# Running sum of three block products in one accumulator bank, at the end of a transformer layer kernel

## The chip, the cores and the metric

The kernel runs on one core of one Trainium2 chip. The engines are TensorE (PE, matrix products into the accumulator memory PSUM), VectorE (DVE, two-input element-wise work), ScalarE (ACT, one-input element-wise work), GpSimd (POOL) and SyncE (SP, which here only issues transfers). Each engine works through its own queue in order, and the queues are kept apart by semaphores. The metric is the device time of one execution in microseconds; times are medians of several runs, and one execution is also recorded by the hardware profiler.

## The reference

One layer on 512 tokens of width 1024, in float32: RMSNorm, a wide projection, three branches (gated linear attention, forgetting attention, attention into 256 memory tokens), merged by gates and projected; then a feed-forward layer and a last RMSNorm. What matters here is the end:

```python
u2 = rmsnorm(h, g_ffn[l])
h = h + jnp.square(jax.nn.relu(u2 @ w_ff1[l])) @ w_ff2[l]     # w_ff1 (1024, 4096), w_ff2 (4096, 1024)
return rmsnorm(h, g_final)
```

## The kernel before

**Precision.** Every float32 operand is split into a high and a low part (`split`, lines 207 to 209: ScalarE casts `hi` on line 208, VectorE subtracts to get `lo` on line 209), and `mm3` (line 154) multiplies by three matmuls: high by high (line 155), high by low (156), low by high (157). Weights pass through `wp`, a pool with three slots each for raw, `hi` and `lo`, so the cast of a tile waits until TensorE has done with the tile three places before.

**Feed-forward layer.** The 4096 hidden channels are worked in four quarters, q = 0 to 3. In each, `first_product` makes the hidden activations, and `second_product` (line 1338) multiplies them by the quarter's rows of `w_ff2` and adds to the result `hN`: four tiles of 128 tokens by 1024. Both are 2 by 2 block products by Winograd's form of Strassen's method: seven block products instead of eight. `C(i, j, t)` is the part of the result in token half i, column half j, tile t of that half, 128 by 512.

**Second product.** The block products are made in the order `SECOND` = 1, 2, 5, 3, 6, 7, 4. Their left factors are sums of activation blocks (`left`, `late_left`), their right factors sums of weight blocks: `factor` (line 1329) lets a GpSimd-issued transfer add the next block in DRAM onto the tile that is in SBUF (`b11`, `b12`) and splits it (`split_b`, line 1153); products 2 and 3 use plain blocks (`ring`). A block product is made for two token tiles t = 0, 1 and two halves of the contraction i = 0, 1: 24 matmuls of 128 by 512, ordered i = 0 (t = 0, then t = 1), then i = 1 (t = 0, then t = 1). Only the very last one (q = 3, n = 4) goes t = 0 with both i first, then t = 1. Each (product, t) has a PSUM bank. Products 1 and 5 stay in two banks each of pool `pa` (tiles `a`, kept in `held`) and are summed there by TensorE over all four quarters; all others get a fresh bank (`mmt`, tile `mm`, four of them) and are read out by `evac` (line 1286):

- products 2 and 3 are added to C(0,0) and C(0,1), product 4 to C(1,0), in every quarter;
- products 6 and 7 are collected in `R6` and `R7` in the first three quarters; R7 is added to C(1,0) and taken from C(1,1) before the last quarter's second product;
- in the last quarter product 1 is copied out by ScalarE, added to C(0,0), and R6 is subtracted from it; at product 6 this gives E (the sum of products 1 and 6 over all quarters, with sign) and G = held product 5 - E. Then C(0,1) += G, C(1,1) += G, C(1,0) += E. Product 7 is taken from C(1,1) and added to C(1,0).

**Finishing.** `finish(t, c, n)` (line 1269) is called when a half row of the result is final. It squares and sums the half on ScalarE; on the first half (n = 0) it multiplies it by the last gain; on the second (n = 1) it forms the reciprocal root (VectorE line 876, GpSimd `pow` line 877), scales both halves (VectorE line 1278, ScalarE line 1280) and stores them from the SP queue (line 1279) and the ScalarE queue (line 1281). Tiles 0 and 1 become final with product 6, tiles 2 and 3 with product 4.

**Order of work.** TensorE's order is the order of the code (`manual_schedule`, line 1470). For all other engines a planner orders the instructions at build time by simulating a timeline, and inserts the waits; `tc.issue_after(x)` makes what follows on the same engine come behind instruction x in that order, without waiting for its end.

Of the kernel before, what the change touches and what calls it, by code (L numbers as in the profile page):

```python
# [9 lines left out]
F32 = mybir.dt.float32  # L10
# [4 lines left out]
ALU = mybir.AluOpType  # L15
AX = mybir.AxisListType

P = 128
# [46 lines left out]
def hybrid_block(ctx, tc, chunks, wst, memT, xN, cols, gffn, gfin, wup, cst, out):  # L65
    nc = tc.nc
# [5 lines left out]
    def nm(s):  # L72
        uid[0] += 1
        return f"{s}_{uid[0]}"
# [10 lines left out]
    def mmt(shape=None):  # L85
        return pmm.tile(shape or [P, 512], F32, tag="mm", name=nm("mm"))

    def at_(shape=None):
        return pa.tile(shape or [P, 512], F32, tag="a", name=nm("a"))

    def f(ap):
        return ap.bitcast(F32)
# [58 lines left out]
    def get_w(key):  # L151
        return split_w(load_w(key))

    def mm3(ps, lh, ll, rh, rl, start, stop):
        nc.tensor.matmul(ps, lh, rh, start=start, stop=False)  # L155
        nc.tensor.matmul(ps, lh, rl, start=False, stop=False)  # L156
        nc.tensor.matmul(ps, ll, rh, start=False, stop=stop)  # L157

    def gT(key, rhi, rlo, evac, n=S):

# [46 lines left out]
    def split(hi, lo, src):  # L207
        nc.scalar.copy(hi, src)  # L208
        return nc.vector.tensor_tensor(lo, src, f(hi), op=ALU.subtract).ins  # L209
# [41 lines left out]
    with pool("front") as fp:  # L251
# [25 lines left out]
        ps = at_()  # L277
# [7 lines left out]
        for j in range(4):  # L285
            for k in (2 * j, 2 * j + 1):
                with tc.issue_after(act):
                    act = nc.scalar.mul(mxh[:, k, :], memr[:, k, :], gmem[:, k:k + 1]).ins
                nc.vector.scalar_tensor_tensor(mxl[:, k, :], memr[:, k, :], gmem[:, k:k + 1], f(mxh[:, k, :]),
                                               op0=ALU.mult, op1=ALU.subtract)  # L290
# [62 lines left out]
        for k in range(KT):  # L353
# [3 lines left out]
            if k in (3, 5):  # L357
                h = k // 5
# [508 lines left out]
    def sumsq(sq, src, t, c, n):  # L867

        nc.scalar.activation(sq, src[:, 512 * c:512 * c + 512], AF.Square, accum_out=hss[:, t, n:n + 1])
        if n == 0:  # L870
            nc.vector.tensor_scalar(hss[:, t, 0:1], hss[:, t, 0:1], 1.0 / D, EPS, op0=ALU.mult, op1=ALU.add)

    def rms_tile(pool_, t):
        ms = pool_.tile([P, 1], F32, tag="ms", name=nm("ms"), bufs=2)
        r = pool_.tile([P, 1], F32, tag="rr", name=nm("rr"), bufs=2)
        nc.vector.tensor_scalar(ms, hss[:, t, 1:2], 1.0 / D, hss[:, t, 0:1], op0=ALU.mult, op1=ALU.add)
        nc.gpsimd.tensor_tensor(r, ms, mhalf[:, :1], op=ALU.pow)
        return r
# [254 lines left out]
    FIRST, SECOND = (1, 2, 5, 6, 3, 7, 4), (1, 2, 5, 3, 6, 7, 4)  # L1133
    with pool("ff") as yp:

        ev, od = ([yp.tile([P, 2, 512], F32, name=f"{n}{i}") for i in range(2)] for n in ("ev", "od"))
        s1 = [yp.tile([P, 512], F32, name=f"s1{i}") for i in range(2)]
        ch, cl = ([yp.tile([P, 4, 512], F32R, name=f"{n}{i}") for i in range(2)] for n in ("ch", "cl"))
        R6, R7 = ([yp.tile([P, 512], F32, name=f"R{n}{t}") for t in range(2)] for n in (6, 7))
        u2s = [yp.tile([P, 3, 4, 256], F32R, name=n) for n in ("u2sh", "u2sl")]  # L1140
        NQ = 4
        held = {}

        def scratch():
            return yp.tile([P, S], F32, tag="sq", name=nm("sq"), bufs=2)

        def sub(to, x, y):
            nc.vector.tensor_tensor(to, x, y, op=ALU.subtract)

        def add(to, x, op=ALU.add):  # L1150
            nc.vector.tensor_tensor(to, to, x, op=op)  # L1151

        def split_b(raw):
            hi, lo = (wp.tile([P, 1024], F32R, tag=g, name=nm(g)) for g in ("hi", "lo"))
            split(hi, lo, raw)
            return hi, lo

        load_n = [0]
# [1 line left out]
        def ring(src):  # L1160
            load_n[0] += 1
            raw = (yp if load_n[0] % 4 == 0 else wp).tile([P, 1024], F32, tag="raw", name=nm("raw"))
            nc.sync.dma_start(raw, src)
            return split_b(raw)
# [6 lines left out]
        def left(i, slot, src):  # L1171
            split(ch[i][:, slot, :], cl[i][:, slot, :], src)

        def late_left(i):

            sub(s1[i], ev[i][:, 1, :], od[i][:, 1, :])
            left(i, 2, s1[i])
            sub(s1[i], ev[i][:, 0, :], s1[i])
            left(i, 3, s1[i])

        def plain_evac(j, ps):
# [87 lines left out]
        def finish(t, c, n):  # L1269

            sumsq(scratch(), hN[t], t, c, n)
            h = [hN[t][:, 512 * g:512 * g + 512] for g in range(2)]
            g_ = [gl[:, 512 * g:512 * g + 512] for g in range(2)]
            if n == 0:
                nc.vector.tensor_tensor(h[c], h[c], g_[c], op=ALU.mult)
            else:
                r = rms_tile(yp, t)
                nc.vector.scalar_tensor_tensor(h[c], h[c], r, g_[c], op0=ALU.mult, op1=ALU.mult)
                nc.sync.dma_start(out[t * P:(t + 1) * P, 512 * c:512 * c + 512], h[c])
                nc.scalar.mul(h[1 - c], h[1 - c], r)  # L1280
                nc.scalar.dma_start(out[t * P:(t + 1) * P, 512 - 512 * c:1024 - 512 * c], h[1 - c])

        def C(i, j, t):
            return hN[2 * i + t][:, 512 * j:512 * j + 512]

        def evac(q, n, t, ps):
            last = q == NQ - 1
            if n == 1 and last:
                x = scratch()
                nc.scalar.copy(x, ps)  # L1290
                add(C(0, 0, t), x)
                sub(R6[t], x, R6[t])
            if n == 2:
                add(C(0, 0, t), ps)
                if last:
                    finish(t, 0, 0)
            if n == 3:
                add(C(0, 1, t), ps)
            if n in (6, 7) and not last:
                R = (R6 if n == 6 else R7)[t]  # L1300
                if q == 0:
                    nc.scalar.copy(R, ps)
                else:
                    add(R, ps)
            if n == 6 and last:
                E, G = R6[t], s1[t]
                sub(E, E, ps)
                sub(G, held[5][t], E)
                add(C(0, 1, t), G)
                finish(t, 1, 1)  # L1310
                add(C(1, 1, t), G)
                add(C(1, 0, t), E)
            if n == 7 and last:
                add(C(1, 1, t), ps, ALU.subtract)
                finish(2 + t, 1, 0)
                add(C(1, 0, t), ps)
            if n == 4:
                add(C(1, 0, t), ps)
                if last:
                    finish(2 + t, 0, 1)  # L1320

        LEFT = {1: 0, 2: 1, 5: 2, 3: 0, 6: 3, 7: 1, 4: 2}

        def load_blocks(q):
# [4 lines left out]
        def factor(q, n, i):  # L1329

            if n in (2, 3):
                return ring(wst[index["B", q, i, {2: "21", 3: "22"}[n]]])
            to, x = {1: (b11, None), 5: (b11, "12"), 6: (b11, "22"), 7: (b12, "22"), 4: (b11, "21")}[n]
            if x is not None:
                nc.gpsimd.dma_start(to[i], wst[index["B", q, i, x]], accum_op=ALU.add)  # L1335
            return split_b(to[i])

        def second_product(q):
            for n in SECOND:
                keep = n in (1, 5)  # L1340
                if not keep:
                    ps = [mmt() for _ in range(2)]
                else:
                    ps = held.setdefault(n, [at_() for _ in range(2)] if q == 0 else None)
                end = q == NQ - 1 and n == SECOND[-1]
                for js in ([[0, 1]] if end else [[0], [1]]):
                    w = {i: [x.rearrange("p (k c) -> p k c", k=2) for x in factor(q, n, i)] for i in js}
                    for t in range(2):
                        for i in js:
                            for k in range(2):  # L1350
                                sl = slice(256 * k + t * P, 256 * k + t * P + P)
                                mm3(ps[t], ch[i][:, LEFT[n], sl], cl[i][:, LEFT[n], sl], w[i][0][:, k, :], w[i][1][:, k, :],
                                    i == k == 0 and not (keep and q), i == k == 1 and (not keep or q == NQ - 1))
                        if js[-1] == 1 and not (keep and q < NQ - 1):
                            evac(q, n, t, ps[t])
                for i in range(2):
                    if n == 1:
                        sub(od[i][:, 0, :], od[i][:, 0, :], s1[i])
                        left(i, 0, od[i][:, 0, :])
                    if n == 2:  # L1360
                        sub(ev[i][:, 1, :], ev[i][:, 0, :], ev[i][:, 1, :])
                        left(i, 1, ev[i][:, 1, :])
                    if n == 5:
                        left(i, 2, od[i][:, 1, :])
# [117 lines left out]
```

## Time and profile before

| | |
|---|---|
| median of 3 runs | 830.68 us (830.3 to 831.02) |
| the profiled execution | 830.25 us, span 828.5 us |
| granted TensorE clock, mean | 0.998 |
| TensorE / VectorE / ScalarE / GpSimd busy | 98% / 73% / 56% / 13% |
| VectorE busy, 810 to 820 us | 10.00 of 10.00 us |
| TensorE busy, 800 to 810, 810 to 820 us | 10.00 and 8.57 us |

The span is what the profiler saw from the first to the last instruction; the rest of the execution's time lies around it. Lines of a timeline give the start in microseconds, the duration, the engine, the line of the code, the operation and its operands; behind them, in brackets, is how long the engine had been idle and what ended that. "x2" means that two such instructions in a row are shown as one line. A line of the chain of waits gives start, duration on the chain, engine and line. Matmuls overlap: the next starts before the one before it has ended.

### The profile page before, as it was taken

To read this page: it belongs to the slowest core of one execution; us is meant where nothing else is said; L and a number is where in the kernel's file an instruction comes from. 1 tells how busy PE (TensorE), PEld (TensorE's weight loads), DVE (VectorE), ACT (ScalarE), POOL (GpSimd) and SP (SyncE) were. 2 spreads that over 40 slices of the span, in tenths; PEclk is the share of its full clock that TensorE was granted. 3 is DMA by queue.
4 is the path that set the end of the run, shared out by engine and by line. 5 is a ranking of instruction groups with operands and counts; after the bars stand their busy time and mean duration, and the time that the engine had idled before them with its cause. 6 is when DMAs were issued, how large, how long until landed. Compare 5 with 4: busy or idle time off the path is not lost.

```text
span 828.5 us, 12438 instructions
## 1 busy us (share of the span) xinstructions
PE 813.4 (98%) x4759; PEld 715.4 (86%) x4759; DVE 603.1 (73%) x946; ACT 460.2 (56%) x721; POOL 105.3 (13%) x129
## 2 busy tenths in 40 slices
PE   8999999999999999999999999999999999999995
PEld 6788888888888888899999889988998899889984
DVE  5856887666455686886576647895689678878897
ACT  7765786653345233544344436775676467637754
POOL 1001100101102020132231100011001100100011
PEclk9999999999999999999999999999999999999999
DMA  9524666689687875667675503978758966896553
GB/s 331 183 100 162 189 186 199 189 215 287 159 247 241 217 236 146 138 181 191 153 200 156 201 28 128 280 159 223 233 175 187 219 217 171 195 255 187 148 89 115
DMA packets 39180, 155.60 MB, mean 188 GB/s; under 512 B 4880, under 2 KB 5840, under 8 KB 37072
## 3 DMA queue, kind: packets, MB, share of 16 engines
q1 hardware_dynamic: 27712, 95.54, 33.5%
q0 software_dynamic: 9328, 54.01, 31.5%
q10 hardware_dynamic: 2080, 5.26, 1.8%
q8 instruction: 37, 0.61, 0.3%
q14 instruction: 23, 0.19, 0.1%
HBM read 152.65 MB, written 31.49 MB: 222 GB/s over the span
## 4 chain that ended last, share of the span: by engine, by line
PE 89%; DVE 5%; DMA 2%; issue 1%; ACT 1%; POOL 0%; ACTq 0%; POOLq 0%; DVEq 0%
PE mm L155 22%; PE mm L156 22%; PE mm L157 22%; PE a L156 5%; PE a L155 5%; PE a L157 5%; DVE lo L209 1%; DVE h L1151 1%; PE a L797 1%; DMA xn<-in_xN_dram 1%; DMA nFb<-dF 1%; DMA memr<-in_memT_dram 1%; PE a L526 1%; PE a L559 1%; DVE wlo L146 1%
## 5 line engine op out<-in xcount | busy, mean ns | idle before, releaser
L155 PE MATMUL mm<-uhi,whi 128*128 128x512 f32 (+1 forms) x352 | 126.1, 358 | 0.0
L157 PE MATMUL mm<-uhi,wlo 128*128 128x512 f32 (+1 forms) x352 | 123.8, 352 | 0.0
L156 PE MATMUL mm<-ulo,whi 128*128 128x512 f32 (+1 forms) x352 | 123.6, 351 | 0.0
L146 DVE TENSOR_TENSOR wlo<-raw,whi 128x1024 fp32r<-128x1024 f32 x68 | 88.1, 1300 | 43.4 <-ACT whi L145 42.8
L145 ACT CAST whi<-raw 128x1024 fp32r<-128x1024 f32 x68 | 71.3, 1050 | 79.3 <-PE mm L156 45.2
L208 ACT CAST hi<-raw 128x1024 fp32r<-128x1024 f32 x65 | 68.2, 1050 | 47.5 <-PE mm L156 32.8
L209 DVE TENSOR_TENSOR lo<-raw,hi 128x1024 fp32r<-128x1024 f32 x65 | 79.5, 1223 | 18.8 <-ACT hi L208 18.8
L157 PEld LDWEIGHTS mm<-uhi,wlo 128*128 128x128 f32 x352 | 66.6, 189 | 9.2
L155 PEld LDWEIGHTS mm<-uhi,whi 128*128 128x128 f32 x352 | 66.7, 189 | 8.3 <-issue 0.3
L156 PEld LDWEIGHTS mm<-ulo,whi 128*128 128x128 f32 x352 | 66.7, 190 | 8.0
L208 ACT CAST hi<-b 128x1024 fp32r<-128x1024 f32 x40 | 41.9, 1048 | 40.9 <-PE mm L157 28.2
L156 PE MATMUL mm<-lo,ch 128*128 128x512 f32 x160 | 62.5, 391 | 0.9 <-DVE lo L209 0.9
L157 PE MATMUL mm<-u2h,lo 128*128 128x256 f32 x224 | 63.4, 283 | 0.0
L156 PE MATMUL mm<-u2l,hi 128*128 128x256 f32 x224 | 63.4, 283 | 0.0
L155 PE MATMUL mm<-u2h,hi 128*128 128x256 f32 x224 | 63.4, 283 | 0.0
L157 PE MATMUL mm<-hi,cl 128*128 128x512 f32 x160 | 62.3, 389 | 0.0
L155 PE MATMUL mm<-hi,ch 128*128 128x512 f32 x160 | 62.2, 389 | 0.0
L209 DVE TENSOR_TENSOR lo<-b,hi 128x1024 fp32r<-128x1024 f32 x40 | 48.9, 1224 | 18.2 <-ACT hi L208 18.2
L1335 POOL DMA_DIRECT2D b<-in_wst_dram x32 | 27.3, 854 | 272.5 <-DVE lo L209 208.7
L155 PE MATMUL mm<-u2sh,hi 128*128 128x256 f32 x168 | 47.5, 283 | 0.0
L156 PE MATMUL mm<-u2sl,hi 128*128 128x256 f32 x168 | 47.5, 283 | 0.0
L157 PE MATMUL mm<-u2sh,lo 128*128 128x256 f32 x168 | 47.5, 283 | 0.0
(406 smaller groups left out, 2134.7 us busy)
## 6 DMA issues: line engine op xcount, KB each, us to landing
raw<-in_wst_dram SPq DMA_DIRECT2D x114, 512.0 KB
b<-in_wst_dram POOLq DMA_DIRECT2D x32, 512.0 KB, 5.5
raw<-T SPq DMA_DIRECT2D x28, 512.0 KB
T<-in_wst_dram POOLq DMA_DIRECT2D x12, 1024.0 KB, 9.0
b<-in_wst_dram SPq DMA_DIRECT2D x16, 512.0 KB
wb<-in_wst_dram POOLq DMA_DIRECT2D x15, 512.0 KB, 5.5
wb<-in_wst_dram SPq DMA_DIRECT2D x8, 512.0 KB
T<-in_wst_dram POOLq DMA_DIRECT2D x6, 512.0 KB, 5.3
```

The lines of the kernel that those rows point to most:

```text
L145: cast = nc.scalar.copy(hi, raw)
L146: low_now[0] = nc.vector.tensor_tensor(lo, raw, f(hi), op=ALU.subtract).ins
L155: nc.tensor.matmul(ps, lh, rh, start=start, stop=False)
L156: nc.tensor.matmul(ps, lh, rl, start=False, stop=False)
L157: nc.tensor.matmul(ps, ll, rh, start=False, stop=stop)
L208: nc.scalar.copy(hi, src)
L209: return nc.vector.tensor_tensor(lo, src, f(hi), op=ALU.subtract).ins
L526: nc.tensor.matmul(ps[:, :w], q, K[e][:, 0, :w], start=True, stop=False)
L559: nc.tensor.matmul(po[:, q0:], vv, PTl[:, c0:c0 + w], start=False, stop=n == 3)
L797: nc.tensor.matmul(ps[:, t, :], kk[:, sl], qq[:, sl], start=True, stop=True)
L1151: nc.vector.tensor_tensor(to, to, x, op=op)
L1335: nc.gpsimd.dma_start(to[i], wst[index["B", q, i, x]], accum_op=ALU.add)
```

## The change

In the last quarter, products 6, 7 and 4 no longer get banks of their own. They are summed by TensorE onto product 1's two banks (`held[1]`, one for each t), without starting a new sum. VectorE reads the banks in between: after product 1 (added to C(0,0)), after product 6 (subtracted from C(0,1)), after product 7 (subtracted from C(1,1)), after product 4 (added to C(1,0)). To make these running sums right:

- the left factor of product 6 changes sign (`late_left`: the last subtraction is turned round; the factor of product 3, which used the same tile, is then a sum);
- in the first three quarters product 6 is subtracted from C(0,1) at once, and also collected, now in R7 together with product 7. R6 is gone;
- product 5's held sum is added to C(0,1) and to C(1,1) at product 3 of the last quarter.

TensorE may write a bank again only when VectorE has read it. `split_b` gets an argument: in the last quarter the `lo` split of the second half (i = 1) of product 7's weights is queued on VectorE behind the read of product 6 for tile 0, and that of product 4's weights behind the read of product 7 for tile 0 (`read`).

`finish` with n = 1 now returns its scaling and stores as a function `store`. For tiles 0 and 1 it is called at once, after product 6's read. For tile 2 it is called after the last sum of tile 3, and its VectorE instruction is queued behind that sum.

```diff
-    def mm3(ps, lh, ll, rh, rl, start, stop):
-        nc.tensor.matmul(ps, lh, rh, start=start, stop=False)
...
+    def mm3(ps, lh, ll, rh, rl, start, stop, on=False):
+        nc.tensor.matmul(ps, lh, rh, start=start, stop=False, skip_group_check=on)
...
-        R6, R7 = ([yp.tile([P, 512], F32, name=f"R{n}{t}") for t in range(2)] for n in (6, 7))
+        R7 = [yp.tile([P, 512], F32, name=f"R7{t}") for t in range(2)]
...
         def add(to, x, op=ALU.add):
-            nc.vector.tensor_tensor(to, to, x, op=op)
+            return nc.vector.tensor_tensor(to, to, x, op=op).ins
 
-        def split_b(raw):
+        def split_b(raw, after=None):
             hi, lo = (wp.tile([P, 1024], F32R, tag=g, name=nm(g)) for g in ("hi", "lo"))
-            split(hi, lo, raw)
+            nc.scalar.copy(hi, raw)
+            with tc.issue_after(after) if after is not None else ExitStack():
+                nc.vector.tensor_tensor(lo, raw, f(hi), op=ALU.subtract)
             return hi, lo
...
-            sub(s1[i], ev[i][:, 0, :], s1[i])
+            sub(s1[i], s1[i], ev[i][:, 0, :])
             left(i, 3, s1[i])
...
                 r = rms_tile(yp, t)
-                nc.vector.scalar_tensor_tensor(h[c], h[c], r, g_[c], op0=ALU.mult, op1=ALU.mult)
...
+                def store():
+                    nc.vector.scalar_tensor_tensor(h[c], h[c], r, g_[c], op0=ALU.mult, op1=ALU.mult)
+                    nc.sync.dma_start(out[t * P:(t + 1) * P, 512 * c:512 * c + 512], h[c])
+                    nc.scalar.mul(h[1 - c], h[1 - c], r)
+                    nc.scalar.dma_start(out[t * P:(t + 1) * P, 512 - 512 * c:1024 - 512 * c], h[1 - c])
+
+                return store
...
         def evac(q, n, t, ps):
             last = q == NQ - 1
-            if n == 1 and last:
-                x = scratch()
-                nc.scalar.copy(x, ps)
-                add(C(0, 0, t), x)
-                sub(R6[t], x, R6[t])
-            if n == 2:
+            if n in (1, 2):
                 add(C(0, 0, t), ps)
-                if last:
+                if n == 2 and last:
                     finish(t, 0, 0)
             if n == 3:
                 add(C(0, 1, t), ps)
-            if n in (6, 7) and not last:
-                R = (R6 if n == 6 else R7)[t]
-                if q == 0:
-                    nc.scalar.copy(R, ps)
+                if last:
+                    add(C(0, 1, t), held[5][t])
+                    add(C(1, 1, t), held[5][t])
+            if n == 6:
+                ins = add(C(0, 1, t), ps, ALU.subtract)
+                if last:
+                    read.setdefault(7, ins)
+                    finish(t, 1, 1)()
+                elif q == 0:
+                    nc.scalar.copy(R7[t], ps)
                 else:
-                    add(R, ps)
-            if n == 6 and last:
-                E, G = R6[t], s1[t]
-                sub(E, E, ps)
-                sub(G, held[5][t], E)
-                add(C(0, 1, t), G)
-                finish(t, 1, 1)
-                add(C(1, 1, t), G)
-                add(C(1, 0, t), E)
+                    add(R7[t], ps)
             if n == 7 and last:
-                add(C(1, 1, t), ps, ALU.subtract)
+                read.setdefault(4, add(C(1, 1, t), ps, ALU.subtract))
                 finish(2 + t, 1, 0)
-                add(C(1, 0, t), ps)
+            elif n == 7:
+                add(R7[t], ps)
             if n == 4:
-                add(C(1, 0, t), ps)
+                ins = add(C(1, 0, t), ps)
                 if last:
-                    finish(2 + t, 0, 1)
-
+                    with tc.issue_after(ins):
+                        for store in stores:
+                            store()
+                        stores[:] = [finish(2 + t, 0, 1)]
+                    if t:
+                        stores[0]()
+
+        read, stores = {}, []
...
-            return split_b(to[i])
+            return split_b(to[i], read.get(n) if i else None)
...
-                if not keep:
+                on, end = q == NQ - 1 and n in (6, 7, 4), q == NQ - 1 and n == SECOND[-1]
+                if on:
+                    ps = held[1]
+                elif not keep:
                     ps = [mmt() for _ in range(2)]
...
-                                    i == k == 0 and not (keep and q), i == k == 1 and (not keep or q == NQ - 1))
+                                    i == k == 0 and not (keep and q or on),
+                                    i == k == 1 and (not keep or q == NQ - 1), on)
...
                     if n == 1:
-                        sub(od[i][:, 0, :], od[i][:, 0, :], s1[i])
+                        add(od[i][:, 0, :], s1[i])
```

More of the change, by code (lines that the diff above doesn't have):

```diff
@@ L152, in get_w @@
         return split_w(load_w(key))
-    def mm3(ps, lh, ll, rh, rl, start, stop):
-        nc.tensor.matmul(ps, lh, rh, start=start, stop=False)
-        nc.tensor.matmul(ps, lh, rl, start=False, stop=False)
-        nc.tensor.matmul(ps, ll, rh, start=False, stop=stop)
+    def mm3(ps, lh, ll, rh, rl, start, stop, on=False):
+        nc.tensor.matmul(ps, lh, rh, start=start, stop=False, skip_group_check=on)
+        nc.tensor.matmul(ps, lh, rl, start=False, stop=False, skip_group_check=on)
+        nc.tensor.matmul(ps, ll, rh, start=False, stop=stop, skip_group_check=on)
     def gT(key, rhi, rlo, evac, n=S):
@@ L1277, in finish @@
                 r = rms_tile(yp, t)
-                nc.vector.scalar_tensor_tensor(h[c], h[c], r, g_[c], op0=ALU.mult, op1=ALU.mult)
-                nc.sync.dma_start(out[t * P:(t + 1) * P, 512 * c:512 * c + 512], h[c])
-                nc.scalar.mul(h[1 - c], h[1 - c], r)
-                nc.scalar.dma_start(out[t * P:(t + 1) * P, 512 - 512 * c:1024 - 512 * c], h[1 - c])
+                def store():
[4 more added lines that the diff above has]
+                return store
         def C(i, j, t):
@@ L1344, in second_product @@
                     ps = held.setdefault(n, [at_() for _ in range(2)] if q == 0 else None)
-                end = q == NQ - 1 and n == SECOND[-1]
                 for js in ([[0, 1]] if end else [[0], [1]]):
```

## The prediction

> **What bounds the kernel now.** I read the page first, then the chain of waits for the last 29 us, and then the timelines of TensorE, VectorE and ScalarE over that stretch.
>
> ```profile
> span 828.5 us, 12438 instructions
> PE 813.4 (98%) x4759; PEld 715.4 (86%) x4759; DVE 603.1 (73%) x946; ACT 460.2 (56%) x721; POOL 105.3 (13%) x129
> PE 89%; DVE 5%; DMA 2%; issue 1%; ACT 1%; POOL 0%; ACTq 0%; POOLq 0%; DVEq 0%
> ```
>
> Over the whole span TensorE is the bound: it is busy 98% of the time and makes 89% of the chain. The change does not alter the number of matmuls, so it can gain only where TensorE stands still or has finished. The chain of waits from 800 us on shows that place:
>
> ```profile
> 804.71 1.06 ACT hi L208
> 805.79 1.23 DVE lo L209
> 807.02 1.20 DVE R L1148 x2
> ...
> 821.17 0.60 DVE h L1151
> ```
>
> From 805.8 us VectorE, not TensorE, sets the end. The timeline of TensorE shows what that costs:
>
> ```profile
> 801.79 0.39 PE L155 MATMUL mm<-hi,ch 128*128 128x512 f32 x1
> ...
> 805.65 0.39 PE L157 MATMUL mm<-hi,cl 128*128 128x512 f32 x1
> ...
> 807.01 0.39 PE L157 MATMUL mm<-hi,cl 128*128 128x512 f32 x1
> 807.24 0.39 PE L155 MATMUL mm<-hi,ch 128*128 128x512 f32 x1
> ...
> 811.09 0.39 PE L157 MATMUL mm<-hi,cl 128*128 128x512 f32 x1
> ...
> 812.67 0.39 PE L155 MATMUL mm<-hi,ch 128*128 128x512 f32 x1
> ...
> 814.03 0.39 PE L155 MATMUL mm<-hi,ch 128*128 128x512 f32 x1
> 815.35 0.50 PE L156 MATMUL mm<-lo,ch 128*128 128x512 f32 x1 [0.93 <-DVE lo L209]
> ...
> 819.11 0.39 PE L157 MATMUL mm<-hi,cl 128*128 128x512 f32 x1
> ```
>
> A block product is 24 matmuls. Product 6 runs from 801.79 to 807.24, so a matmul starts every 5.45 / 24 = 0.227 us and its result is there 0.39 us after its start. Product 7 begins at 807.24 and product 4, the last, at 812.67. In product 4 the eighth matmul waits for a `lo` split that VectorE did late. Without a wait the 24th would start at 812.67 + 23 x 0.227 = 817.89; it starts at 819.11, so 1.2 us are lost. It ends at 819.11 + 0.39 = 819.50. The timeline of VectorE for the same stretch:
>
> ```profile
> 802.56 1.29 DVE L1151 TENSOR_TENSOR h<-h,mm 128x512 f32<-128x512 f32 x2
> 803.76 1.23 DVE L209 TENSOR_TENSOR lo<-b,hi 128x1024 fp32r<-128x1024 f32 x1
> 805.79 1.23 DVE L209 TENSOR_TENSOR lo<-b,hi 128x1024 fp32r<-128x1024 f32 x1 [0.81 <-ACT hi L208]
> 806.94 1.28 DVE L1148 TENSOR_TENSOR R<-R,mm 128x512 f32<-128x512 f32 x2
> ...
> 811.67 2.49 DVE L1151 TENSOR_TENSOR h<-h,s 128x512 f32<-128x512 f32 x4
> 814.08 1.22 DVE L209 TENSOR_TENSOR lo<-b,hi 128x1024 fp32r<-128x1024 f32 x1
> ...
> 821.09 0.68 DVE L1151 TENSOR_TENSOR h<-h,mm 128x512 f32<-128x512 f32 x1
> ```
>
> The four `h` sums at 811.67 stand ahead of the split at 814.08, for which TensorE waits, and the queue is still not empty at the end: the last product's second half is complete at 819.50 and is read only at 821.09, a backlog of 1.59 us.
>
> **The change part by part.** Times are for one profiled execution of 830.25 us (span 828.5 and 1.75 around it); the median of the runs is 830.68, 0.43 more, and I subtract the gain from the median.
>
> 1. *Tail sums removed.* Two 512-column sums in a row take 1.28 us, so each holds VectorE for 0.60 us. In the last quarter, product 6 is evacuated by five VectorE operations per token tile before (E, G, and sums into three quadrants of the result) and by one after; product 7 by two before and one after. That is 2 x (4 + 1) = 10 operations or 6.0 us out of the stretch after 805.8 us. The backlog of 1.59 us and the late split both fit in that. So the last split is done in time and the 1.2 us come back, and the last read starts when the last matmul ends: 1.59 us less 0.05 us for the hand-over (an estimate by the split that ends at 815.30 and the matmul that follows at 815.35).
>
> 2. *Sums added earlier.* At product 3 the last quarter gets two more sums per tile (product 5 into two quadrants), 4 x 0.60 = 2.4 us, and product 1 loses its two R subtractions, 1.2 us (and two ScalarE copies). VectorE was full up to 804.99 and then idle 0.81 us, so by the rows above the split at 803.76 moves to at most 1.2 us later and ends near 806.2. It is needed when the second matmul of product 7 starts, 807.47. Cost nothing; without that cover up to 1.2 us.
>
> 3. *The reads between.* New: product 7 may write the bank of tile t only after VectorE has read the running sum that product 6 left there, and product 4 only after the read of product 7's. Behind the waiting matmul stands all of TensorE, and behind TensorE the `hi` casts of ScalarE, which wait for weight slots. Each bank's sum is complete while the other tile's six matmuls run. Read 6 of tile 0 is ready at 805.65 + 0.39 = 806.04 and due at 807.24; of tile 1 ready at 807.40, due 807.24 + 6 x 0.227 = 808.60; read 7 of tile 0 ready 811.48, due 812.67; of tile 1 ready 812.84, due 12 matmuls after 812.67, at 815.39. With 0.68 us for a read, the first three have about 0.5 us to spare and the fourth 1.9 us. No row shows such a wait. Its bounds: nothing, if VectorE is free at the three moments, and 3 x 0.78 = 2.3 us if a split has just started each time (1.13 us until the next can start, less 0.51 to spare, and 0.16 us for the restart: the hand-over, and a first matmul of 0.50 us where 0.39 is usual). The change itself places two splits behind a read (`issue_after`): the second split of product 7 behind read 6 of tile 0, the second of product 4 behind read 7 of tile 0. The first of these ends about 806.2 + 0.6 + 1.13 = 807.95 and read 6 of tile 1 follows, to 808.6: just on time or slightly late. I take 0.25 us, near the lower end, since only that one of the reads has a split placed ahead of it.
>
> 4. *Finish and stores.* For the first two token tiles the final sum is now complete with read 6, so their norm (ScalarE square, GpSimd power, VectorE scale) and their stores on the SP and ScalarE queues can move from the last microseconds to about 807 to 812 us, while product 7 runs. Per tile the scale is one VectorE operation beside two small ones, moved, not added, into a stretch that has lost 6.0 us. The GpSimd queue has the transfers of product 4's weights ahead of these powers, as before; nobody but the stores waits for them. For tile 2 the store is put behind the last sum of tile 3 on VectorE: its 0.75 us run beside the ScalarE square of tile 3, so they cost nothing. The rest of the tail is the same chain:
>
> ```profile
> 821.81 0.63 ACT L869 ACTIVATE sq<-h 128x512 f32<-128x512 f32 x1 [1.20 <-DVE h L1151]
> 822.86 0.99 POOL L877 TENSOR_TENSOR rr<-ms,cst_s 128x1 f32<-128x1 f32 x1 [0.33 <-DVE ms L876]
> 824.63 0.37 ACTq L1281 DMA_DIRECT2D out_dram<-h  x1
> L877 POOL TENSOR_TENSOR rr<-ms,cst_s x4: 548/554/987, 816.2 to 822.9; 128x1 f32<-128x1 f32 x4
> ```
>
> From the start of the last sum to the end of the span it took 828.5 - 821.09 = 7.41 us. The power took 0.99 us there against a median of 0.55; half of that, 0.2 us, I count as gained. Of the 3.87 us from the last issue to the end a part may be queueing behind tile 2's store just ahead of it; the two stay close, so I count an estimated 0.2 us. Bounds for this part: 0 to 1.0 us.
>
> 5. *Earlier quarters.* Product 6 now updates the result and R7 where it only updated R6, and product 7 joins R7: two VectorE operations more per quarter (two copies fewer on ScalarE in the first). Second quarter, VectorE around product 6:
>
> ```profile
> 649.77 1.28 DVE L1151 TENSOR_TENSOR R<-R,mm 128x512 f32<-128x512 f32 x2
> 651.35 1.23 DVE L209 TENSOR_TENSOR lo<-b,hi 128x1024 fp32r<-128x1024 f32 x1 [0.30 <-ACT hi L208]
> 654.07 1.23 DVE L209 TENSOR_TENSOR lo<-b,hi 128x1024 fp32r<-128x1024 f32 x1 [1.49 <-ACT hi L208]
> ```
>
> Idle 0.30 + 1.49 = 1.79 us takes the 1.2 us; a split is used two half products (5.4 us) after its slot came free. Cost nothing; if that cover were gone, 3 x 1.2 = 3.6 us. The flipped sign (one subtraction turned round, one made a sum) and the 4 KB of R6 that move later tiles of this pool down change no count of operations; by the order of the code the moved tiles are written after the last readers of what lay there before. Cost nothing.
>
> Sum: 1.2 - 0.25 + 1.54 + 0.4 = 2.9 us less. 830.68 - 2.9 = 827.8 (profiled 827.35, span about 825.6).
>
> **The rivals.** (a) *The reads come late.* The rule that speaks against the change is one of shared banks: a read and the next product's writes exclude each other. By the upper bound of part 3 the three tight reads cost 2.3 us instead of 0.25, and 2.05 of the gain is gone: 827.8 + 2.05 = 829.9, within what counts as no change. For it: of the stretch of VectorE shown above only 0.81 us up to 808 is idle. Against it: ten operations fewer there.
> The Trainium skill, "PSUM — Partial Sum Buffer", section "PSUM bank collisions raise a hardware error", says that the chip does not arbitrate between two engines on one bank, so software has to keep them apart with semaphores by bank. By that, every read between is a wait of TensorE, and with nothing beside it the sum would be 4 x 0.68 = 2.7 us of stalls, which is the whole gain; the two banks taken in turn are what the trace sets against it, and no row of before shows such a wait.
>
> (b) *Slower: each tight read stands behind a split whose cast is still to come.* VectorE works in order. If at each of the three moments the next split is queued ahead of the read and waits for its `hi` cast, the read comes after cast, split and itself: as for this cast of product 4's first weights on ScalarE:
>
> ```profile
> 807.43 1.05 ACT L208 CAST hi<-b 128x1024 fp32r<-128x1024 f32 x1 [1.67 <-PE mm L157]
> ```
>
> It ends at 808.48, so the split at about 809.6 and the read at 810.3, where 808.60 was due: 1.7 us lost. Three such are 5.1 us in place of 0.25: 827.8 + 4.85 = 832.7. It decides from 2.9 + 0.25 + 1.66 = 4.8 us of stalls on, 1.6 us a boundary. Against it: the edges put two of those splits behind the read. For it: the first split of product 4 has no such edge.
>
> (c) *More than forecast.* No stall at all, the power always 0.55 us, and the last store not queueing: 1.2 + 1.54 + 1.0 = 3.7: 827.0.
>
> **How the numbers follow.** What a measurement of this kernel can tell from no change is 0.2%, 1.66 us: faster means under 829.0, slower over 832.3. My forecast has 0.58, (c) 0.14, (a) 0.16, (b) 0.12. Faster is then 0.72, no change 0.16, slower 0.12. The forecast's own range is 827.1 to 829.0 (stalls 0 to 1.2, tail as above). The range for 8 in 10 reaches from a little under (c), 826.5, to the far side of (a), 830.3: (b), and a few hundredths at either end, are left out.
>
> **What would show it.** Right: no wait of over 0.3 us of TensorE for `lo` in product 4; the last VectorE sum starting within 0.2 us of the last matmul's end; stores of tiles 0 and 1 before 814 us; the last matmul ending near 818.5. Wrong: waits of TensorE for an `h` sum at the start of product 7 or 4 adding up to over 1 us; a split of product 7 late; a gap of TensorE before 800 us that before does not have; or a last sum still 1 us behind the last matmul.

## The result and the profile after

The changed kernel takes 828.11 us (median of 7 runs, 827.21 to 829.16) against 830.68 us before (7 runs); the ratio is 0.9967, 95% interval 0.9956 to 0.9979. That is 2.6 us less, and the whole interval lies beyond the 0.2% (1.66 us) up to which the prediction speaks of no change; 827.8 us were forecast. The profiled execution took 828.11 us, its span is 826.3 us. The page after:

```profile
span 826.3 us, 12441 instructions
PE 813.3 (98%) x4759; PEld 715.4 (87%) x4759; DVE 603.3 (73%) x946; ACT 457.9 (55%) x717; POOL 104.8 (13%) x129
PE 91%; DVE 4%; DMA 2%; issue 1%; ACT 1%; POOL 0%; ACTq 0%; POOLq 0%; DVEq 0%
```

VectorE does as much work as before (603.3 against 603.1 us, 946 instructions both times). What changed is when. TensorE's timeline from product 6 on:

```profile
802.04 0.39 PE L155 MATMUL a<-hi,ch 128*128 128x512 f32 x1
...
807.25 0.39 PE L157 MATMUL a<-hi,cl 128*128 128x512 f32 x1
807.69 0.47 PE L155 MATMUL a<-hi,ch 128*128 128x512 f32 x1
...
808.92 0.39 PE L157 MATMUL a<-hi,cl 128*128 128x512 f32 x1
809.33 0.50 PE L155 MATMUL a<-hi,ch 128*128 128x512 f32 x1
...
813.54 0.39 PE L155 MATMUL a<-hi,ch 128*128 128x512 f32 x1
...
818.76 0.39 PE L157 MATMUL a<-hi,cl 128*128 128x512 f32 x1
```

All these matmuls now write the banks `a`. The wait in product 4 is gone (23 matmuls in 818.76 - 813.54 = 5.22 us, 0.227 us each). Two small ones are new: the first matmul of product 7 starts at 807.69 instead of 802.04 + 24 x 0.227 = 807.48, and its seventh, the first of tile 1, 0.41 us after the sixth instead of 0.23. From the start of product 6 to the start of the last matmul it takes 16.72 us; without any wait it would be 71 x 0.227 = 16.1 us, and before it was 819.11 - 801.79 = 17.32 us. VectorE's timeline shows who is waited for, and the end:

```profile
801.92 1.29 DVE L1151 TENSOR_TENSOR h<-h,mm 128x512 f32<-128x512 f32 x2
803.33 1.23 DVE L1157 TENSOR_TENSOR lo<-b,hi 128x1024 fp32r<-128x1024 f32 x1
804.47 3.07 DVE L1151 TENSOR_TENSOR h<-h,a 128x512 f32<-128x512 f32 x5
807.45 1.22 DVE L1157 TENSOR_TENSOR lo<-b,hi 128x1024 fp32r<-128x1024 f32 x1
808.59 0.68 DVE L1151 TENSOR_TENSOR h<-h,a 128x512 f32<-128x512 f32 x1
...
811.28 1.42 DVE L1282 SCALAR_TENSOR_TENSOR h<-h,rr,gl 128x512 f32<-128x512 f32 x2 [0.62 <-POOL rr L877]
812.61 0.68 DVE L1151 TENSOR_TENSOR h<-h,a 128x512 f32<-128x512 f32 x1
...
819.19 0.69 DVE L1151 TENSOR_TENSOR h<-h,a 128x512 f32<-128x512 f32 x1 [0.96 <-PE a L157]
```

Of the five sums at 804.47 the first four are product 5's held sums, the fifth is the first read between (product 6, tile 0); it ends at 807.54, and TensorE starts at 807.69. The read of tile 1 follows behind the split at 807.45, ends at 809.27, and TensorE starts at 809.33. The read of product 7 for tile 0 (812.61) stands behind the two scales of tiles 0 and 1, which waited for GpSimd's power, and ends at 813.29. It holds nobody up, since TensorE comes to product 4 at 813.54. But without the two waits before, TensorE would have come at 802.04 + 48 x 0.227 = 812.94, ahead of where this read now ends. At the end VectorE has been idle for 0.96 us when the last matmul's sum is complete (818.76 + 0.39 = 819.15), and the last read starts 0.04 us later; before, it came 1.59 us late.

Where the 2.2 us between the two spans are, in order (the last matmul's own 0.39 us, the same in both, is left out):

| stretch | before, us | after, us | after - before |
|---|---|---|---|
| start to one matmul of the attention, at 142.73 / 143.31 | 142.73 | 143.31 | +0.58 |
| from there to product 3 of the last quarter (796.03 / 796.60) | 653.30 | 653.29 | -0.01 |
| product 3 to product 6 | 5.76 | 5.44 | -0.32 |
| product 6 to the start of the last matmul | 17.32 | 16.72 | -0.60 |
| end of the last matmul to the start of the last sum | 1.59 | 0.04 | -1.55 |
| last sum to the end of the span | 7.41 | 7.11 | -0.30 |

The first row lies far ahead of anything that the change touches. It is by such an amount that one execution differs from another: the kernels below are edited only behind this place, and the profiled execution of one reaches it 1.27 us later than before (144.00) and of another 0.37 us earlier (142.36). So the change itself is worth 2.8 us in the profile, from product 3 to the end (32.47 against 29.70 us), and this stretch is what the experiments are compared by; the seven whole times of one kernel lie 2 us apart.

### The profile page after: what moved, and what is told of

The parts are those of the page before. It is cut to its first block, busy times and chain, and to the rows that moved or that the text cites. A ratio compares the mean times of both kernels' runs of the same rounds, so it can differ in the third digit from the quotient of the medians.

```text
span 826.3 us, 12441 instructions
## 1 busy us (share of the span) xinstructions
PE 813.3 (98%) x4759; PEld 715.4 (87%) x4759; DVE 603.3 (73%) x946; ACT 457.9 (55%) x717; POOL 104.8 (13%) x129
## 4 chain that ended last, share of the span: by engine, by line
PE 91%; DVE 4%; DMA 2%; issue 1%; ACT 1%; POOL 0%; ACTq 0%; POOLq 0%; DVEq 0%
PE mm L155 23%; PE mm L156 23%; PE mm L157 23%; PE a L156 5%; PE a L155 5%; PE a L157 5%; PE a L797 1%; DMA xn<-in_xN_dram 1%; DMA memr<-in_memT_dram 1%; PE a L526 1%; PE a L559 1%; DVE wlo L146 1%; DVE h L1151 1%; PE a L558 1%; PE a L527 0%
## 5 line engine op out<-in xcount | busy, mean ns | idle before, releaser
L156 PE MATMUL mm<-lo,ch 128*128 128x512 f32 x136 | 52.9, 389 | 0.0
L157 PE MATMUL mm<-hi,cl 128*128 128x512 f32 x136 | 52.9, 389 | 0.0
L155 PE MATMUL mm<-hi,ch 128*128 128x512 f32 x136 | 52.9, 389 | 0.0
```

Of the source, the lines that this page charges most:

```text
L155: nc.tensor.matmul(ps, lh, rh, start=start, stop=False, skip_group_check=on)
L156: nc.tensor.matmul(ps, lh, rl, start=False, stop=False, skip_group_check=on)
L157: nc.tensor.matmul(ps, ll, rh, start=False, stop=stop, skip_group_check=on)
```

## The experiments

**Six sums left out of the kernel before.** Is the gain VectorE's shorter queue, or the sum in one bank? This kernel leaves out the sums of E and G into C(1,0) and C(1,1) and one of the two sums of product 7, so half of its result lacks those parts.

```diff
--- before
                 add(C(0, 1, t), G)
                 finish(t, 1, 1)
-                add(C(1, 1, t), G)
-                add(C(1, 0, t), E)
...
                 finish(2 + t, 1, 0)
-                add(C(1, 0, t), ps)
```

> The kernel before with six VectorE sums of the last quarter left out (E and G into C(1,1) and C(1,0) at product 6, product 7 into C(1,0)), 3.6 us of VectorE work; the result is then incomplete in the lower half. Products 6, 7 and 4 keep their own banks, so there is no running sum, no read between and no store put off. Theory 1 (the gain is VectorE's shorter queue at the end): no wait for a split in product 4, the last sum within 0.2 us of the last matmul's end, about 2.7 us less than before, 827.9. Theory 2 (the gain needs the sums in one bank on TensorE): within 0.5 us of before, 830.7. Theory 3 (the gain is the earlier stores of tiles 0 and 1, which leave the transfer engines free at the end): the stretch from the last sum to the end of the span shrinks from 7.4 us by 1 us or more, the rest stays.

Measured: 827.73 us, ratio to before 0.9967 (0.9957 to 0.9978), the same ratio as that of the change. The timeline of VectorE in this kernel (the split for product 4's second half, and the last sum):

```profile
811.73 1.22 DVE L209 TENSOR_TENSOR lo<-b,hi 128x1024 fp32r<-128x1024 f32 x1
...
818.37 0.69 DVE L1151 TENSOR_TENSOR h<-h,mm 128x512 f32<-128x512 f32 x1 [0.64 <-PE mm L157]
```

The split comes 2.35 us earlier than before, TensorE needs 16.09 us from product 6 to the last matmul, and the last sum starts 0.03 us after the last matmul's end. Theory 1 holds, in both its signs. From product 3 to the end it takes 29.60 us, against 29.70 in the changed kernel. Theory 2 falls: no product is summed on another here, and the gain is there all the same. Theory 3 falls too: the stretch after the last sum takes 825.7 - 818.37 = 7.33 us, 0.08 less than before.

**Six sums put back into the changed kernel.**

```diff
--- after
                 if last:
                     read.setdefault(7, ins)
+                    with tc.issue_after(ins):
+                        for _ in range(3):
+                            extra = add(s1[t], held[5][t])
+                    spare.append(extra)
                     finish(t, 1, 1)()
...
-                read.setdefault(4, add(C(1, 1, t), ps, ALU.subtract))
+                with tc.issue_after(spare[0]), tc.issue_after(spare[1]):
+                    ins = add(C(1, 1, t), ps, ALU.subtract)
+                read.setdefault(4, ins)
```

> The changed kernel with six extra VectorE sums of the same size (3.6 us) on a tile that nobody reads any more, put between the reads of product 6 and the first read of product 7. Theory 1 (VectorE's queue): from the durations in the profile of the changed kernel the second read of product 6 comes 0.6 us later, the first read of product 7 ends about 1.65 us after it is due, both on TensorE's path; 2.2 us more, 830.3. Theory 2 (sums in one bank): the bank sums are untouched, 828.1 to 828.6.

Measured: 830.31 us, ratio to before 1.0000 (0.9990 to 1.0009): in whole times the gain is gone. From product 3 to the end it takes 31.92 us, 2.2 more than the changed kernel and 0.55 less than before. TensorE's timeline in this kernel, the first matmuls of tile 1 in product 7 and of product 4:

```profile
810.60 0.50 PE L155 MATMUL a<-hi,ch 128*128 128x512 f32 x1 [0.61 <-DVE h L1151]
...
816.32 0.47 PE L155 MATMUL a<-hi,ch 128*128 128x512 f32 x1 [1.34 <-DVE h L1151]
```

From product 6 to the last matmul it takes 18.90 us, 2.18 more than the changed kernel; 2.2 were worked out. Here TensorE waits at the banks, so a late read does stop it. The time is lost in another place than before: the splits are not late, and the last sum starts 0.04 us after the last matmul's end.

**No edges on the splits.**

```diff
--- after
-            return split_b(to[i], read.get(n) if i else None)
+            return split_b(to[i])
```

> The changed kernel without the two edges that put the second split of products 7 and 4 behind a read. The planner then puts both splits ahead of the read. Theory 1: read 6 of tile 0 ends about 1.2 us after it is due and read 7 of tile 0 about 1 us, so the stalls of TensorE from product 6 to the end go from 0.6 to about 2.1 us; 1.5 us more, 829.6. If reads between are hidden anyway (their waits cost nothing): no change, 828.1.

Measured: 829.68 us; the ratio to before is 0.9999 (0.9989 to 1.0009), so the time is no longer to be told from before. From product 3 to the end it takes 31.25 us, which is between the changed kernel (29.70) and before (32.47). VectorE and TensorE in this kernel:

```profile
806.01 1.22 DVE L1157 TENSOR_TENSOR lo<-b,hi 128x1024 fp32r<-128x1024 f32 x1
807.15 1.27 DVE L1151 TENSOR_TENSOR h<-h,a 128x512 f32<-128x512 f32 x2
```

```profile
807.97 0.47 PE L155 MATMUL a<-hi,ch 128*128 128x512 f32 x1 [1.18 <-ACT hi L1155]
...
814.09 0.47 PE L155 MATMUL a<-hi,ch 128*128 128x512 f32 x1 [0.42 <-DVE h L1151]
```

The split now stands ahead of the read, which ends at 807.83, and product 7 starts at 807.97, 1.34 us after it could have (801.19 + 5.44). The profile puts that wait down to a ScalarE cast that had long been done; the read of the bank, 0.14 us ahead of the matmul, fits. From product 6 to the last matmul it takes 18.19 us, 1.47 more than with the edges. So more than half of the change's gain hangs on two edges in VectorE's queue.

**Tile 2 stored at once.**

```diff
--- after
-                    with tc.issue_after(ins):
-                        for store in stores:
-                            store()
-                        stores[:] = [finish(2 + t, 0, 1)]
-                    if t:
-                        stores[0]()
+                    finish(2 + t, 0, 1)()
```

> The changed kernel with the store of tile 2 not put off: its scale on VectorE then stands ahead of the last sum of tile 3 and waits for GpSimd's power. Theory 1: the last sum starts about 0.4 us later, all else the same; 0.3 to 0.4 us more, 828.5. If putting the store off is what emptied the queue at the end (rival): the backlog of before, 1.5 us, comes back, 829.6.

Measured: 827.94 us, ratio to before 0.9972 (0.9962 to 0.9982). In the profile the scale of tile 2 stands ahead of the last sum, which starts 0.41 us after the last matmul's end instead of 0.04; from product 3 to the end it takes 30.06 us against 29.70. That is the 0.3 to 0.4 us of theory 1. Whole times do not show it (828.5 was expected), and the backlog of 1.5 us does not come back. The last matmul, then VectorE in this kernel:

```profile
818.04 0.39 PE L157 MATMUL a<-hi,cl 128*128 128x512 f32 x1
```

```profile
818.17 0.75 DVE L1282 SCALAR_TENSOR_TENSOR h<-h,rr,gl 128x512 f32<-128x512 f32 x1 [0.66 <-POOL rr L877]
818.84 0.68 DVE L1151 TENSOR_TENSOR h<-h,a 128x512 f32<-128x512 f32 x1
```

**The held sums later, the edge later, and each alone.** These ask what the 0.6 us of new waits are, and try to win them back.

```diff
--- after, the two sums moved
                 if last:
                     add(C(0, 1, t), held[5][t])
-                    add(C(1, 1, t), held[5][t])
...
                 read.setdefault(4, add(C(1, 1, t), ps, ALU.subtract))
+                add(C(1, 1, t), held[5][t])
```

```diff
--- the edge behind tile 1's read (second and third run)
-                    read.setdefault(7, ins)
+                    read[7] = ins
```

> The changed kernel with the two sums of product 5 into C(1,1) moved from product 3 to behind the read of product 7: 1.2 us of VectorE ahead of the first read between are gone. Theory 1 (each read is late by what VectorE has queued ahead of it): read 6 of tile 0 starts when its bank is complete and ends 0.5 us before it is due; the split placed behind it then ends 0.6 us earlier, and read 6 of tile 1 is in time too. From the start of product 6 to the start of the last matmul 16.1 to 16.2 us instead of 16.7, the floor being 71 x 0.227 = 16.1; about 0.5 us less in all, 827.6. If TensorE's 0.6 us are the price of a read between itself, however early it is done: 16.7 us and 828.1.

> As the run with the two sums moved, and the second split of product 7 put behind the read of tile 1 instead of tile 0. Theory 1: 16.1 to 16.2 us from the start of product 6 to the start of the last matmul, with both reads of product 6 ending 0.5 us before they are due; 0.5 us less than the changed kernel, 827.6. A price of the read itself: 16.7 us, 828.1.

> The changed kernel with the split put behind the read of tile 1 alone, the sums of product 5 where they are. Theory 1: the first wait of TensorE (0.2 us and a slower first matmul) stays, since the four sums still stand ahead of read 6 of tile 0; the second goes. 16.4 us from the start of product 6 to the start of the last matmul; 0.3 us less, 827.8. A price of the read itself: 16.7 us.

| | product 6 to the last matmul, us | product 3 to the end, us | median, us | ratio to before (95%) |
|---|---|---|---|---|
| changed kernel | 16.72 | 29.70 | 828.11 | 0.9967 (0.9956 to 0.9979) |
| sums moved | 16.19 | 29.20 | 828.25 | 0.9965 (0.9951 to 0.9978) |
| sums moved, edge behind tile 1 | 16.68 | 29.59 | 827.61 | 0.9962 (0.9949 to 0.9974) |
| edge behind tile 1 alone | 16.93 | 30.00 | 828.52 | 0.9973 (0.9962 to 0.9984) |

Each ratio is to runs of before on the same occasion. For the three new kernels these took 831.08 us in the median, so their own medians are not to be set beside 828.11 us.

The first came out as expected in the profile: VectorE is idle when the bank is complete, both reads of product 6 end in time, and TensorE loses 0.1 us in all. VectorE and TensorE of this kernel, the two reads and the start of product 7 for each tile:

```profile
805.32 0.69 DVE L1151 TENSOR_TENSOR h<-h,a 128x512 f32<-128x512 f32 x1 [0.58 <-PE a L157]
805.93 1.22 DVE L1157 TENSOR_TENSOR lo<-b,hi 128x1024 fp32r<-128x1024 f32 x1
807.07 0.68 DVE L1151 TENSOR_TENSOR h<-h,a 128x512 f32<-128x512 f32 x1
```

```profile
806.48 0.39 PE L155 MATMUL a<-hi,ch 128*128 128x512 f32 x1
...
807.84 0.46 PE L155 MATMUL a<-hi,ch 128*128 128x512 f32 x1
```

The read of tile 0 ends at 806.01, 0.47 us before TensorE's turn at 806.48, and costs nothing. So a read between has no price of its own when it comes in time. A late one costs what it is late, the 0.06 to 0.15 us from its end to the next matmul, and about 0.1 us because that matmul takes 0.47 or 0.50 us instead of 0.39.

The other two missed their numbers (16.68 for 16.1 to 16.2, 16.93 for 16.4). With the later edge the second wait in product 7 goes (with the sums moved, both go), but a new one opens at product 4. In the second run, VectorE and then TensorE:

```profile
810.82 1.41 DVE L1282 SCALAR_TENSOR_TENSOR h<-h,rr,gl 128x512 f32<-128x512 f32 x2 [0.33 <-POOL rr L877]
812.15 0.68 DVE L1151 TENSOR_TENSOR h<-h,a 128x512 f32<-128x512 f32 x1
```

```profile
812.98 0.47 PE L155 MATMUL a<-hi,ch 128*128 128x512 f32 x1 [0.29 <-DVE h L1151]
```

The read of product 7 for tile 0 stands behind the two scales of tiles 0 and 1, which waited for GpSimd's power. Pushing one split back pushed this work back too: the scales start 9.18 us after product 6 does, against 8.45 with the sums moved alone. In the third run it is the same read and the same matmul:

```profile
812.64 0.68 DVE L1151 TENSOR_TENSOR h<-h,a 128x512 f32<-128x512 f32 x1
```

```profile
813.47 0.47 PE L155 MATMUL a<-hi,ch 128*128 128x512 f32 x1 [0.26 <-DVE h L1151]
```

Counted from the start of product 6, the read comes 0.2 us later than in the changed kernel, and TensorE would come to product 4 0.3 us sooner (813.06), since one wait before it is gone. So the wait has in part only moved. The expectations had followed the reads of product 6 only. The version with the sums moved is the best in the profile (0.5 us better than the change from product 3 to the end), but its time cannot be told from the changed kernel's: the two ratios to before overlap almost wholly.

## Why the prediction was right

The time (827.8 forecast, 828.11 measured) and the direction came out, and by the mechanism named: VectorE's queue set the end, and the change shortened it.

- **Part 1, tail sums removed.** Right. The wait of 1.2 us in product 4 is gone, and the last sum starts 0.04 us after the last matmul (0.05 assumed), a gain of 1.55 us. The run without six sums shows the same two signs with nothing else of the change in it. Six sums put back take the gain away again, though by waits at the banks and not by a late split or a backlog.
- **Part 2, sums added earlier: "cost nothing".** Wrong, by a little. The split that I looked at was in time (804.56, needed 807.7). But the four sums came behind it and ahead of the first read between. Its bank was ready at 805.89 + 0.39 = 806.28, and the read began at about 806.86. That is the 0.2 us wait at 807.69. Moving two of the sums away removes it. The mistake was to ask of the added work only what it does to the work that was there before, not to the new read of part 3.
- **Part 3, the reads between: 0.25 us.** The right mechanism, too small a size: it cost 0.62 us (16.72 less 16.1). The read of tile 1 was late by the split placed ahead of it, as worked out; the read of tile 0 was late by part 2, which was not counted; and each wait makes the next few matmuls slower (0.47 and 0.50 us for the first). The reads of product 7 cost nothing here, but that of tile 0 ends after the time at which an undelayed TensorE would have needed it (813.29 against 812.94).
- **Part 4, the tail: 0.4 us.** 0.30 measured. GpSimd's power took 0.55 us instead of 0.99. The prediction counted half of this as if by chance, but it goes with the order on VectorE. In the two kernels where VectorE scales tile 2 beside this power (before, and six sums left out) it took 0.99 us; in the seven others VectorE is idle then, and it took 0.55. The scale of before, which the 0.99 us power at 822.86 overlaps:

```profile
822.69 0.74 DVE L1278 SCALAR_TENSOR_TENSOR h<-h,rr,gl 128x512 f32<-128x512 f32 x1
```

It was also wrong that nobody but the stores waits for the powers: the scales of tiles 0 and 1, which wait for them, stand ahead of the read of product 7. The store gave nothing: from the last issue to the end it takes 3.89 us (822.41 to 826.3) against 3.87, although the stores of tiles 0 and 1 were issued from 812 us on. ScalarE's last square started 0.15 us after the sum, 0.11 later than before. From the timelines of ScalarE, GpSimd, ScalarE's queue and SP's queue of the changed kernel (the last line shows four stores as one, the first of them at 812.06):

```profile
820.03 0.63 ACT L869 ACTIVATE sq<-h 128x512 f32<-128x512 f32 x1 [0.41 <-DVE h L1151]
821.08 0.55 POOL L877 TENSOR_TENSOR rr<-ms,cst_s 128x1 f32<-128x1 f32 x1 [2.22 <-DVE ms L876]
822.41 0.37 ACTq L1285 DMA_DIRECT2D out_dram<-h  x1
812.06 10.71 SPq L1283 DMA_DIRECT2D out_dram<-h  x4
```

- **Part 5, earlier quarters: nothing.** Right: 653.29 against 653.30 us over that stretch, with the extra sums in it. The first quarter got four of them and not two (product 6 is subtracted and product 7 added, for each tile), eight in all; so VectorE's count comes out the same, 946.
- **Not counted:** the small wait in product 3 before (0.32 us), which went with the two subtractions that product 1 lost, 1.2 us ahead of product 3's splits. The run without six sums keeps these two, and keeps the wait (5.76 us for product 3, as before). It made up for the 0.37 us by which part 3 was short. That the total came out so near (2.9 us forecast, 2.8 in the profile) is to this extent luck.
- **Rival (a), reads late,** happened in part, 0.6 of its 2.3 us. The Trainium skill, "PSUM — Partial Sum Buffer", section "PSUM bank collisions raise a hardware error", has software guard a bank by semaphores. The trace agrees that the reads bind TensorE: it waited for them at two of four places here and lost 2.8 us (16.1 to 18.90) by them in the run with the sums put back. But with two banks taken in turn they are free when they come in time.
- **Rival (b), slower,** did not happen. In the run without edges the splits do stand ahead of the reads of tile 0; the stalls are 2.1 us (18.19 less 16.1), less than half of the 4.8 that the rival needs. But the same sums in the same banks with two splits placed otherwise give away 1.5 of the 2.8 us.
- **Rival (c), more than forecast,** did not happen: the power was short, but the reads cost 0.62 us and the store gave nothing.
- **The range.** The forecast's own range, 827.1 to 829.0 us, does not follow from its terms: stalls of 0 to 1.2 us and a tail of 0 to 1.0 us give 826.9 to 829.1.

## What to carry to other kernels

When TensorE is busy 98% of the time, look at the queue that ends last: here ten VectorE sums (6.0 us) fewer at the end were worth most of 2.8 us, although VectorE's total work stayed the same. A running sum in one bank saves evacuation sums, but makes each read a wait of TensorE; with two banks taken in turn a read is free as long as it ends before TensorE is back at its bank. So list what stands ahead of each read in its queue, including what the change itself adds, and follow it to the next reads too: a wait that is taken away at one can come back at another. Take a microsecond's worth of change from the stretch that it touches, not from the whole time: the front alone differed by more than 1 us between executions.

## What was not expected of the hardware

The last store takes 3.9 us from its issue to the end of the span whether half of the eight stores are issued 4 to 7 us or 9 to 10 us ahead of it: 3.87 us before, 3.89 us after. What makes up these 3.9 us was not tried.

GpSimd's power of 128 values takes 0.55 us, but four of those in this stretch took 0.99 to 1.44: the last one of before and of the run without six sums, and that of tile 0 in the two runs with the sums moved. Each began while VectorE was at work on a scale or a split, and each ended about 0.42 us after that instruction (before: scale to 823.43, power to 823.85). Beside VectorE sums that read an accumulator bank it took 0.55 to 0.57 us. One power that began together with a scale, at 814.47 in the run without six sums, took 0.55 us as well; the cause was not tried.
